# The first stage of an encoder trunk: norm by token, inputs on two queues, idle products, and a second home for modulation weights

## The chip, the core and the metric

The kernel runs on one core of one Trainium2 chip. The time is the device time of one execution in microseconds; a kernel's time is the median over its runs. The profile is of one such execution. Engines are named as in the profile: PE (TensorE, matrix products), PEld (its weight loads), DVE (VectorE), ACT (ScalarE), POOL (GpSimd), SP (SyncE, which issues most of the transfers).

## What is computed

The input is x (256 frames of 1024 channels) and a vector c of 1024. Two layers follow, each of three sub-layers: a SwiGLU feed-forward of 2816, a mixer (pooling in layer 0, short convolution in layer 1), and a second feed-forward. Each sub-layer is wrapped by a norm and a modulation that depends on c. All is float32.

```python
def rms_norm(x, g):
    y = xf * lax.rsqrt(jnp.mean(xf * xf, axis=-1, keepdims=True) + RMS_EPS)
    return (y * g).astype(x.dtype)

cond = jax.nn.silu(c)
for i in range(DEPTH):
    mod = (cond @ ada_w[i] + ada_b[i]).reshape(B, N_SUB, N_MOD, D_MODEL)
    shift, scale, gate = mod[:, :, 0], mod[:, :, 1], mod[:, :, 2]
    h = rms_norm(x, norm_g[i, 0]) * (1 + scale[:, 0]) + shift[:, 0]
    x = x + 0.5 * gate[:, 0] * swiglu(h, ffn_w_in[i, 0], ffn_w_out[i, 0])
    ...
return rms_norm(x, final_g)
```

## The kernel before

**Layout.** Channels lie on the 128 partitions, in 8 blocks (`KB`), and frames along the row: `x[:, k]` is block k of all 256 frames. All weights come from one array, `wall`, in units of 128 x 2048 float32 (1 MB), in the order in which the program asks for them. `raw_unit` takes a slot of a pool (tag `raw`, `NRAW` = 4 slots; a few units go to other tiles under tags of their own, `hi` and `lo`) and issues one transfer from SyncE (line 199). SyncE works through its transfers in order: each waits until its slot has been read for the last time, and all behind it wait with it. So SyncE runs ahead of the other engines by as many units as there are slots.

**Products in three parts.** A weight unit is split into two float32r tiles: `high` copies the unit to `hi` on ScalarE (line 239), `low` subtracts it again on VectorE to get `lo` (line 246). The activations are split likewise, into `hh` and `hl`. `mm3` makes one product of float32 quality out of three fast ones: hi with hh, lo with hh, hi with hl. `high(n)` and `low(n)` see to it that n units ahead of the one in use are split; `take` hands out the next one. The order of the work on each engine is the order of the program, written out by hand (`manual_schedule`).

**Modulation.** A modulation value is a dot product of a weight row with `cond`, made on VectorE (line 262, one dot for 128 channels, 1024 elements a partition). `mod_dots` makes the dots of a unit and finishes them (1 + scale times norm_g, half a gate). `ada_first(kb)` fetches the unit with scale and shift of block kb for the first sub-layer. All other modulation units go through `ada_unit`: `spread` deals them out over the steps of a feed-forward, and `slot` or `ada_next` fetches and works off one.

**The first stage** (lines 873 to 889 and `ffn_start`, from line 582). Four parts of x are squared on ScalarE into the buffer `hf` (8 blocks of 257 columns) and added on VectorE; cond is spread over the partitions by two products and put through Silu. `rstd_of` sums the squares over the partitions with a 128 x 256 product, takes the root on ScalarE and the reciprocal of 128 x 256 elements on VectorE (line 334). Then eight rounds follow, one for each block of the sum over channels. Round kb makes the block's modulation (two dots), forms h in `modulated` (t = x * scale * rstd on VectorE, line 359; t + shift on ScalarE, line 360; hl on VectorE, line 361), splits the block's weight unit in two halves (lines 618 and 623), and adds 48 products to eight PSUM banks, which hold 8 of the 22 column pairs of the first feed-forward. Round 0 takes its weight and its h unsplit, in plain float32, 16 products; its split into hh and hl is made in round 1. The second half of a round's `lo` and its products are put behind the dots of the next round (`second`).

**Behind it** all eight banks are full. `swiglu_pair` (from line 555: Silu on ScalarE, product gf and its split on VectorE) frees them two by two; product 8 needs the first. Column pairs 8 to 21 follow, one unit and 48 products each, then the second matrix (11 units, `out_product`), with the modulation units of the later part dealt out in between. `hf` isn't used from the end of the rounds until `pool_shift_by_token`, late in `out_product`, where the pooling mixer begins to use it.

Of the kernel before, what the change touches and what calls it, by code (L numbers as in the profile page):

```python
# [9 lines left out]
F32 = mybir.dt.float32  # L10
F32R = mybir.dt.float32r
AF = mybir.ActivationFunctionType
ALU = mybir.AluOpType
# [104 lines left out]
def trunk(ctx: ExitStack, tc: tile.TileContext, calls, consts: bass.AP, c_in: bass.AP,  # L118
# [16 lines left out]
    def mm(dst, w, m, start, stop):  # L135
        PE.matmul(dst, w, m, start=start, stop=stop, skip_group_check=True)  # L136
# [10 lines left out]

    eps = one.tile([P, LEAD], F32, name="eps")[:, :1]
    G.memset(eps, EPS)
    cond = one.tile([P, D], F32, name="cond")  # L150
    nc.sync.dma_start(cond[0:1], c_in)
    x = one.tile([P, KB, T], F32, name="x")
    for p in range(4):
        at = slice(2 * p, 2 * p + 2)
        nc.sync.dma_start(x[:, at], x_in[:, at])
# [23 lines left out]
    def table(func):  # L179

        tabs.append(wk.tile([P, 1], F32, tag="tab", name=f"tab{len(tabs)}"))
        S.activation(tabs[-1], eps, func)
# [9 lines left out]
    gh = one.tile([P, FC, T], F32R, name="gh")  # L192
    gl = one.tile([P, FC, T], F32R, name="gl")

    def raw_unit(*call, tag="raw"):
        u = len(calls)
        calls.append(call)
        t = wp.tile([P, UNIT], F32, tag=tag, name=f"raw{u}", bufs=NRAW if tag == "raw" else NSPLIT)
        nc.sync.dma_start(t, wall[u])
        return t  # L200
# [34 lines left out]
    def high(n, parts=1):  # L235

        for _, raw, hi, _ in next_of("hi", n):
            for at in spans(parts) if hi else ():
                S.copy(hi[:, at], raw[:, at])  # L239

    def low(n, parts=1):

        high(n, parts)
        for _, raw, hi, lo in next_of("lo", n):
            for at in spans(parts) if hi else ():
                V.tensor_sub(lo[:, at], raw[:, at], hi[:, at].bitcast(F32))  # L246
# [17 lines left out]
    def mod_dots(layer, sub, mod, w, lo):  # L264

        key, n = (layer, sub, mod), w.shape[1]
        if key not in mods:
            mods[key] = one.tile([P, KB], F32, name=f"mod{layer}{sub}{mod}")
        b = ada_col(layer, sub, mod) + lo
        for i in range(n):  # L270
            dot(mods[key][:, lo + i : lo + i + 1], w[:, i], cst[:, b + i : b + i + 1])
        mod_finish(key, lo, n)

    def mod_finish(key, lo, n):
# [7 lines left out]
        elif mod == GATE and layer == 0:  # L282
            V.tensor_mul(m, m, cst[:, C_PS + lo : C_PS + lo + n])

    def ada_unit(layer, sub, mod, q):
# [3 lines left out]
    def ada_first(kb):  # L289
        raw = raw_unit("ada0", kb).rearrange("p (m n) -> p m n", m=2)  # L290
        mod_dots(0, 0, SCALE, raw[:, 0:1], kb)
        mod_dots(0, 0, SHIFT, raw[:, 1:2], kb)

    ada_todo = []
    slots = {}
# [58 lines left out]
    def modulated(layer, sub, k, rstd, to):  # L354


        scale, shift = (mods[layer, sub, m][:, k : k + 1] for m in (SCALE, SHIFT))
        t = wk.tile([P, T], F32, tag="t", name=f"t{layer}{sub}{k}", bufs=4)
        V.scalar_tensor_tensor(t, x[:, k], scale, rstd, ALU.mult, ALU.mult)
        S.activation(to[:, k, :T], t, AF.Identity, bias=shift)  # L360
# [205 lines left out]
    def swiglu_early(pds, rstd, name, split):  # L566
        for at in range(0, len(pds), 2):
# [11 lines left out]
            for c in cs:  # L579
                V.tensor_sub(gl[:, c], ab[c][1][0], gh[:, c].bitcast(F32))  # L580

    def ffn_start(rstd, name):

        banks = [bank(f"{name}b{c}") for c in range(NFIRST)]
        half = NFIRST // 2

        def product(kb, w, cs):
            for c in cs:
                for s in range(2):
                    mm3(banks[c][:, s], (w[0][:, c, s], w[1][:, c, s]), h_pair(kb),  # L590
                        kb == 0 and s == 0, kb == KB - 1)

        second = lambda: None
        for kb in range(KB):
            if kb:
                ada_first(kb)
            call, raw, hi, lo = unit(kb)
            if hi is None:
                modulated(0, 0, kb, rstd, hf)
                second()  # L600
                low(1)
                w = take("ffn_first", "p (c s n) -> p c s n", c=NFIRST, s=2)
# [4 lines left out]
                def second(kb=kb):  # L607
                    S.copy(hh[:, kb, :T], hf[:, kb, :T])
                    V.tensor_sub(hl[:, kb], hf[:, kb, :T], hh[:, kb, :T].bitcast(F32))

                continue
            low_part = modulated(0, 0, kb, rstd, hh)
            second()
            low_part()
            high(1, 2)
            done["lo"] += 1
            at, bt = spans(2)
            V.tensor_sub(lo[:, at], raw[:, at], hi[:, at].bitcast(F32))
            w = take("ffn_first", "p (c s n) -> p c s n", c=NFIRST, s=2)
            product(kb, w, range(half))  # L620

            def second(kb=kb, w=w, raw=raw, hi=hi, lo=lo):
                V.tensor_sub(lo[:, bt], raw[:, bt], hi[:, bt].bitcast(F32))
                product(kb, w, range(half, NFIRST))

        second()
# [101 lines left out]
    def pool_means():  # L728
        S.copy(mh[:, :, 0, :EDGE], cst[:, C_E:C_M].rearrange("p (g v) -> p g v", g=4))
# [5 lines left out]
        V.tensor_mul(acc[:, :, :n], acc[:, :, :n], at)  # L735

    def pool_shift_by_token():
        pool_means()
# [133 lines left out]

    table(AF.Silu)
    sq2 = [hf[:, 2 * p : 2 * p + 2, :T] for p in range(4)]
    for p in range(4):
        S.activation(sq2[p], x[:, 2 * p : 2 * p + 2], AF.Square)
        if p:
            V.tensor_add(sq2[0], sq2[0], sq2[p])
    for p in range(2):
        b = bank(f"c{p}").rearrange("p a t -> p (a t)")  # L880
        half = slice(p * 512, (p + 1) * 512)
        PE.matmul(b, ones[0:1], cond[0:1, half], start=True, stop=True)
# [3 lines left out]
    V.tensor_add(sqs["a"], sq2[0][:, 0], sq2[0][:, 1])  # L886
# [79 lines left out]
```

## Time and profile before

| what | us |
| --- | --- |
| median of 3 runs | 863.17 |
| the runs | 862.32, 863.17, 872.11 |
| the profiled execution | 863.46 |
| its span, first to last instruction | 861.5 |

How to read the rows. A row of the timeline has the start and length in us, the engine, the line of the kernel, the operation, what it writes and reads (by tile names, without buffer numbers), and in brackets how long the engine sat idle before it and what ended that. A row of the waits reads: who waited, for whom, us in total, times, longest. A row of the windows has a stretch, its length, and for each engine the busy time with the number of instructions in it. The chain that ended last is followed back from the last instruction: at each step to what released it. The transfers of the weights have one line, 199, written `raw<-wall`. A busy PE isn't PE at its peak: the ends of its products are modelled, so their starts are what counts.

### The profile page before, as it was taken

Reading aid. Unit: us, or ns where it says so; the run is one execution under the profiler, and the core shown is the slowest. Engines: PE = TensorE matmul, PEld = TensorE weight load, DVE = VectorE, ACT = ScalarE, POOL = GpSimd, SP = SyncE. Lnnn points to the kernel's source line nnn. Section 1 sums busy time; section 2 is a strip of 40 time slices with the busy share of each in tenths; the row PEclk is TensorE's granted clock in tenths of the full one; section 3 lists DMA queues with packets and bytes.
Section 4 is the critical chain, followed back from the end, with each engine's and each line's share of the span. In section 5 each row is a group of like instructions: output and inputs, shape, how many; then the busy total and the mean of one; then the engine's idle time right before and its main releaser. Section 6 shows DMA issues by size and latency. Waiting matters only on the chain.

```text
span 861.5 us, 16344 instructions
## 1 busy us (share of the span) xinstructions
PE 841.8 (98%) x6940; PEld 822.8 (96%) x6940; DVE 714.6 (83%) x1018; ACT 418.3 (49%) x538; POOL 8.4 (1%) x25
## 2 busy tenths in 40 slices
PE   4999999999999999999999999999999999999997
PEld 2999999999899999999999999999999999999886
DVE  6989999877889987878888988879887789755784
ACT  5355455343655444446644444356444756444422
POOL 3000000000000000000000000000000000000000
PEclk9999999999999999999999999999999999999999
DMA  8898899989548998886389989983465449954601
GB/s 343 335 344 322 301 350 379 370 347 385 178 165 320 372 341 321 350 310 237 105 331 350 377 310 337 363 321 148 161 228 180 190 145 343 331 192 165 224 22 49
DMA packets 33338, 235.59 MB, mean 273 GB/s; under 512 B 3697, under 2 KB 3825, under 8 KB 4978
## 3 DMA queue, kind: packets, MB, share of 16 engines
q1 hardware_dynamic: 33266, 234.56, 73.6%
q8 instruction: 54, 0.88, 0.4%
q14 instruction: 18, 0.15, 0.0%
HBM read 233.49 MB, written 1.05 MB: 272 GB/s over the span
## 4 chain that ended last, share of the span: by engine, by line
PE 85%; DVE 7%; DMA 5%; ACT 1%; issue 1%; SPq 0%; ACTq 0%
PE accf L136 21%; PE f01b L136 13%; PE f10b L136 13%; PE f11b L136 11%; PE acco L136 7%; PE f00b L136 4%; DMA raw<-wall 4%; PE pcv L136 4%; DVE raw L262 3%; PE accc L136 3%; DVE lo L246 2%; PE pe L136 2%; PE pb L136 2%; PE f01a L136 1%; PE f11a L136 1%; PE accz L136 1%
## 5 line engine op out<-in xcount | busy, mean ns | idle before, releaser
L239 ACT CAST hi<-raw 128x2048 fp32r<-128x2048 f32 (+1 forms) x151 | 263.9, 1762 | 132.5 <-DMA raw<-wall 77.5
L246 DVE TENSOR_TENSOR lo<-raw,hi 128x2048 fp32r<-128x2048 f32 (+1 forms) x137 | 298.9, 2194 | 33.1 <-ACT hi L239 32.9
L262 DVE CUSTOM_DVE_ANT_0 raw<-raw,cond,cst 128x1024 f32<-128x1024 f32 x144 | 179.6, 1281 | 12.5 <-DMA raw<-wall 12.2
L136 PE MATMUL accf<-gh,hi 128*128 128x256 f32 x528 | 145.9, 276 | 0.0
L136 PE MATMUL accf<-gh,lo 128*128 128x256 f32 x528 | 145.9, 276 | 0.0
L136 PE MATMUL accf<-gl,hi 128*128 128x256 f32 x528 | 145.8, 276 | 0.0
L136 PEld LDWEIGHTS accf<-gh,lo 128*128 128x128 f32 x528 | 99.1, 188 | 0.2
L136 PEld LDWEIGHTS accf<-gh,hi 128*128 128x128 f32 x528 | 99.1, 188 | 0.0
L136 PEld LDWEIGHTS accf<-gl,hi 128*128 128x128 f32 x528 | 99.1, 188 | 0.0
L136 PE MATMUL f00b<-hh,lo 128*128 128x256 f32 x336 | 93.1, 277 | 1.2 <-DVE lo L246 0.8
L136 PE MATMUL f00b<-hh,hi 128*128 128x256 f32 x336 | 93.1, 277 | 0.4 <-DVE gf L560 0.4
L136 PE MATMUL f00b<-hl,hi 128*128 128x256 f32 x336 | 92.8, 276 | 0.0
L136 PE MATMUL f11b<-hh,lo 128*128 128x256 f32 (+1 forms) x320 | 88.5, 277 | 0.3 <-DVE lo L246 0.3
L136 PE MATMUL f11b<-hh,hi 128*128 128x256 f32 (+1 forms) x320 | 88.4, 276 | 0.0
L136 PE MATMUL f11b<-hl,hi 128*128 128x256 f32 x320 | 88.4, 276 | 0.0
L136 PE MATMUL f10b<-hh,lo 128*128 128x256 f32 x320 | 88.3, 276 | 0.0
L136 PE MATMUL f10b<-hh,hi 128*128 128x256 f32 x320 | 88.3, 276 | 0.0
L136 PE MATMUL f10b<-hl,hi 128*128 128x256 f32 x320 | 88.3, 276 | 0.0
L136 PE MATMUL f01b<-hl,hi 128*128 128x256 f32 x304 | 84.6, 278 | 0.0
L136 PE MATMUL f01b<-hh,hi 128*128 128x256 f32 x304 | 84.2, 277 | 0.0
L136 PE MATMUL f01b<-hh,lo 128*128 128x256 f32 x304 | 83.9, 276 | 0.0
L136 PEld LDWEIGHTS f00b<-hh,lo 128*128 128x128 f32 x336 | 63.1, 188 | 1.8 <-DVE lo L246 1.0
(234 smaller groups left out, 1856.5 us busy)
## 6 DMA issues: line engine op xcount, KB each, us to landing
raw<-wall SPq DMA_DIRECT2D x221, 1024.0 KB, 6.0
x<-xt SPq DMA_DIRECT2D x4, 256.0 KB, 4.1
out<-x SPq DMA_DIRECT2D x4, 256.0 KB, 2.1
rows<-fg SPq DMA_DIRECT2D x1, 512.0 KB, 8.3
cst<-consts SPq DMA_DIRECT2D x1, 176.0 KB, 4.8
cond<-cvec SPq DMA_DIRECT2D x1, 4.0 KB
```

What stands on the lines that cost most here:

```text
L136: PE.matmul(dst, w, m, start=start, stop=stop, skip_group_check=True)
L239: S.copy(hi[:, at], raw[:, at])
L246: V.tensor_sub(lo[:, at], raw[:, at], hi[:, at].bitcast(F32))
L262: V.tensor_tensor_reduce(w, w, cond, 1.0, init, ALU.mult, ALU.add, out)
```

## The change

1. **Inputs on two queues.** The parts of x with odd numbers and the constants are issued by ScalarE, the others by SyncE as before.
2. **Squares.** Two of the four parts are squared on VectorE. The four are added pairwise.
3. **Norm by token.** `rstd_by_token` makes the sum of squares with two one-column products, so that root and reciprocal have one column for 128 frames. The result is brought back along the row: a diagonal matrix (made once on GpSimd, scaled on ScalarE) is multiplied by `ones` (1/1024, against the 1024 on the diagonal) into a PSUM bank.
4. **x over rms by itself.** `normalised` multiplies x by rstd into `hf`: block 0 before the rounds, the other seven in four operations in round 0. `modulated_first` then makes scale and shift in one operation on ScalarE, in place; `split_first` makes hh and hl. The operation t on VectorE is gone.
5. **Order of a round.** First half of hi on ScalarE; the dots; Identity and hh on ScalarE; second half of hi; on VectorE the first half of lo, hl, products, second half of lo, products. Nothing is put off to the next round. hh and hl of block 0 are made at the end of round 1.
6. **Idle products.** `keep_busy` puts 8, 2 and 3 products of 128 columns, whose result isn't used, between the steps of the norm.
7. **Tables.** The Silu table, once loaded behind the norm's root, is loaded behind the rounds.
8. **Modulation units in hf.** From the end of the rounds to `pool_shift_by_token`, every second modulation unit goes to the first 2048 columns of `hf` instead of a slot.

```diff
     for p in range(4):
         at = slice(2 * p, 2 * p + 2)
-        nc.sync.dma_start(x[:, at], x_in[:, at])
+        (nc.scalar if p % 2 else nc.sync).dma_start(x[:, at], x_in[:, at])
     cst = one.tile([P, C_N], F32, name="cst")
-    nc.sync.dma_start(cst, consts)
+    nc.scalar.dma_start(cst, consts)
...
+    def home():
+        if not spare["on"]:
+            return None
+        spare["turn"] += 1
+        return hf.rearrange("p k t -> p (k t)")[:, :UNIT] if spare["turn"] % 2 else None
+
     def ada_unit(layer, sub, mod, q):
-        raw = raw_unit("ada", layer, sub, mod, q).rearrange("p (b n) -> p b n", b=2)
+        raw = raw_unit("ada", layer, sub, mod, q, home=home()).rearrange("p (b n) -> p b n", b=2)
         mod_dots(layer, sub, mod, raw, 2 * q)
...
+    def normalised(ks, rstd):
+        n = ks.stop - ks.start
+        at = bass.AP(rstd.tensor, rstd.offset, [rstd.ap[0], [0, n], rstd.ap[1]])
+        V.tensor_mul(hf[:, ks, :T], x[:, ks], at)
+
+    def modulated_first(k):
+        scale, shift = (mods[0, 0, m][:, k : k + 1] for m in (SCALE, SHIFT))
+        S.activation(hf[:, k, :T], hf[:, k, :T], AF.Identity, bias=shift, scale=scale)
+
+    def split_first(k):
+        S.copy(hh[:, k, :T], hf[:, k, :T])
+        return lambda: V.tensor_sub(hl[:, k], hf[:, k, :T], hh[:, k, :T].bitcast(F32))
...
         for kb in range(KB):
             if kb:
-                ada_first(kb)
+                w_ada = ada_first_weights(kb)
             call, raw, hi, lo = unit(kb)
+            at, bt = spans(2)
+            if hi is not None:
+                S.copy(hi[:, at], raw[:, at])
+            if kb:
+                for m, mod in enumerate((SCALE, SHIFT)):
+                    mod_dots(0, 0, mod, w_ada[:, m : m + 1], kb)
+            modulated_first(kb)
...
             if hi is None:
...
+                for ks in (slice(1, 2), slice(2, 4), slice(4, 6), slice(6, 8)):
+                    normalised(ks, rstd)
                 continue
...
+            low_part = split_first(kb)
+            S.copy(hi[:, bt], raw[:, bt])
+            V.tensor_sub(lo[:, at], raw[:, at], hi[:, at].bitcast(F32))
             low_part()
...
             product(kb, w, range(half))
+            V.tensor_sub(lo[:, bt], raw[:, bt], hi[:, bt].bitcast(F32))
+            product(kb, w, range(half, NFIRST))
+            if kb == 1:
+                split_first(0)()
+
+        spare["on"] = True
+        table(AF.Silu)
         low(1)
         high(2)
...
+    squares(0)
+    squares(1)
     for p in range(2):
...
         PE.matmul(b, ones[0:1], cond[0:1, half], start=True, stop=True)
+        if p == 0:
+            squares(2)
         S.activation(cond[:, half], b, AF.Silu, scale=float(D))
     table(AF.Sqrt)
+    squares(3)
+    idle = bank("idle")
+
+    def keep_busy(n):
+        for _ in range(n):
+            PE.matmul(idle[:, 0, :P], ones, ones, start=True, stop=True)
+
+    keep_busy(8)
+    V.tensor_add(sq2[1], sq2[1], sq2[0])
+    V.tensor_add(sq2[3], sq2[3], sq2[2])
+    V.tensor_add(sq2[1], sq2[1], sq2[3])
     sqs["a"] = wk.tile([P, T], F32, tag="sq", name="sqs", bufs=3)
-    V.tensor_add(sqs["a"], sq2[0][:, 0], sq2[0][:, 1])
-    rstd = rstd_of("s")
-    table(AF.Silu)
-    ada_first(0)
+    V.tensor_add(sqs["a"], sq2[1][:, 0], sq2[1][:, 1])
+    w_first = ada_first_weights(0)
+    mod_dots(0, 0, SCALE, w_first[:, 0:1], 0)
+
+    by_token_rstd = rstd_by_token("s")
+    mod_dots(0, 0, SHIFT, w_first[:, 1:2], 0)
+    keep_busy(2)
...
+    for b in range(2):
+        cut = slice(b * P, (b + 1) * P)
+        S.activation(diag[:, cut], unit_matrix, AF.Copy, scale=by_token_rstd[:, b : b + 1])
+        PE.matmul(rstd[:, cut], ones, diag[:, cut], start=b == 0, stop=True, skip_group_check=True)
+    keep_busy(3)
+    normalised(slice(0, 1), rstd)
```

More of the change, by code (lines that the diff above doesn't have):

```diff
@@ L149, in trunk @@
     G.memset(eps, EPS)
+    unit_matrix = wk.tile([P, T], F32, tag="sa", name="unit")[:, :P]
+    G.memset(unit_matrix, 0.0)
+    G.affine_select(unit_matrix, unit_matrix, [[-1, P]], ALU.not_equal, float(D), base=0, channel_multiplier=1)
     cond = one.tile([P, D], F32, name="cond")
@@ L193, in trunk, with raw_unit @@
     gl = one.tile([P, FC, T], F32R, name="gl")
-    def raw_unit(*call, tag="raw"):
+    def raw_unit(*call, tag="raw", home=None):
         u = len(calls)
         calls.append(call)
+        if home is not None:
+            nc.sync.dma_start(home, wall[u])
+            return home
         t = wp.tile([P, UNIT], F32, tag=tag, name=f"raw{u}", bufs=NRAW if tag == "raw" else NSPLIT)
@@ L283, in mod_finish, with ada_first_weights @@
             V.tensor_mul(m, m, cst[:, C_PS + lo : C_PS + lo + n])
+    spare = {"on": False, "turn": 0}
+    def home():
[3 more added lines that the diff above has]
+        return hf.rearrange("p k t -> p (k t)")[:, :UNIT] if spare["turn"] % 2 else None
     def ada_unit(layer, sub, mod, q):
-        raw = raw_unit("ada", layer, sub, mod, q).rearrange("p (b n) -> p b n", b=2)
+        raw = raw_unit("ada", layer, sub, mod, q, home=home()).rearrange("p (b n) -> p b n", b=2)
         mod_dots(layer, sub, mod, raw, 2 * q)
[L289 to L292, printed above, removed]
+    def ada_first_weights(kb):
+        return raw_unit("ada0", kb).rearrange("p (m n) -> p m n", m=2)
     ada_todo = []
@@ L591, in product @@
                         kb == 0 and s == 0, kb == KB - 1)
-        second = lambda: None
         for kb in range(KB):
             if kb:
-                ada_first(kb)
+                w_ada = ada_first_weights(kb)
             call, raw, hi, lo = unit(kb)
+            at, bt = spans(2)
[5 more added lines that the diff above has]
+            modulated_first(kb)
+            done["hi"] += 1
+            done["lo"] += 1
+            w = take("ffn_first", "p (c s n) -> p c s n", c=NFIRST, s=2)
             if hi is None:
[L599 to L602, printed above, removed]
                 for c in range(NFIRST):
@@ L874, in trunk, with squares @@
     sq2 = [hf[:, 2 * p : 2 * p + 2, :T] for p in range(4)]
[L875 to L878, printed above, removed]
+    def squares(p):
+        xp = x[:, 2 * p : 2 * p + 2]
+        if p % 2:
+            V.tensor_mul(sq2[p], xp, xp)
+        else:
+            S.activation(sq2[p], xp, AF.Square)
+    squares(0)
+    squares(1)
     for p in range(2):
@@ L882, in trunk @@
         PE.matmul(b, ones[0:1], cond[0:1, half], start=True, stop=True)
+        if p == 0:
+            squares(2)
         S.activation(cond[:, half], b, AF.Silu, scale=float(D))
     table(AF.Sqrt)
[L885 to L889 removed]
+    squares(3)
[7 more added lines that the diff above has]
+    V.tensor_add(sq2[1], sq2[1], sq2[3])
+    sqs["a"] = wk.tile([P, T], F32, tag="sq", name="sqs", bufs=3)
+    V.tensor_add(sqs["a"], sq2[1][:, 0], sq2[1][:, 1])
[4 more added lines that the diff above has]
+    keep_busy(2)
+    diag = wk.tile([P, T], F32, tag="sd", name="diag", bufs=1)
+    rstd = bank("rstds")[:, 0]
+    for b in range(2):
[4 more added lines that the diff above has]
+    normalised(slice(0, 1), rstd)
     steady = [4] * (LAST - 2)
```

15 lines of the change are left out of this document (1 added, 14 removed).

## The prediction, made before the changed kernel was run

> **What bounds the kernel now.** I read the page first, then the waits of PE, then the chain that ended last in order of time.
>
> ```profile
> PE 841.8 (98%) x6940; PEld 822.8 (96%) x6940; DVE 714.6 (83%) x1018; ACT 418.3 (49%) x538; POOL 8.4 (1%) x25
> ```
> ```profile
> PE f00b L136 <- ACT hf L360: 5.8, 1, 5.8
> ...
> PE f00b L136 <- DVE lo L246: 0.8, 1, 0.8
> PE f00b L136 <- DVE gf L560: 0.4, 1, 0.4
> PE f00b L136 <- DVE lo L623: 0.4, 1, 0.4
> ```
> ```profile
> 88.40 2.30 DVE lo L246
> 90.75 7.07 DMA raw<-wall
> ...
> 104.69 38.27 PE f00b L136 x335
> ```
> Lines are start, length and what the time went to. From 104.69 us the chain is PE, stage after stage; ahead of it fetches (DMA raw<-wall) and VectorE alternate. What the change can win is therefore the time until PE begins, what PE loses while it runs slowly, and the three waits before 105 us. Whatever arrives earlier at 105 us arrives earlier at the end, as long as VectorE and the fetches keep up.
>
> PE's own pace is seen in two stretches of the first product block (32 records, f00b<-hf,raw) and in one behind it (columns: the stretch and its length, PE and PE's weight loads with the records in it, the granted clock, the DMA engines' busy share, GB/s; the third stretch has VectorE and ScalarE between):
>
> ```profile
> 16.46:20.89 4.43, 4.43 (x10) 3.53 (x11) 1.00 1.03 436
> 21.27:25.59 4.32, 4.32 (x22) 3.80 (x21) 1.00 0.75 305
> ```
> ```profile
> 26.04:55.90 29.86, 29.86 (x264) 29.76 (x263) 0.00 (x0) 0.00 (x0) 1.00 0.93 343
> ```
> The granted-clock column says 1.00 throughout, yet the same instruction takes 0.43 us in the first stretch (4.43/10) and 0.216 in the second (20 begin in it). The slow start costs some 2.3 us. Behind it one fp32r product takes 29.86/263 = 0.1135 us, so a round of 48 takes PE 5.45 us.
>
> **The start, step by step.** Before:
>
> ```profile
> 2.42 3.75 PE L882 MATMUL c<-cond,ones 1*128 1x512 f32 x4 [2.42 <-DMA cond<-cvec]
> ...
> 3.50 56.19 SPq L199 DMA_DIRECT2D raw<-wall  x20
> ...
> 5.96 0.69 DVE L878 TENSOR_TENSOR hf<-hf 128x512 f32<-128x512 f32 x1 [2.88 <-ACT hf L876]
> ...
> 7.46 0.63 ACT L876 ACTIVATE hf<-x 128x512 f32<-128x512 f32 x1 [0.20 <-DMA x<-xt]
> ...
> 8.86 0.53 DVE L886 TENSOR_TENSOR sqs<-hf 128x256 f32<-128x256 f32 x1
> 9.07 1.28 ACT L182 ACT_TABLE_LOAD   x1
> ...
> 11.21 1.75 DVE L334 RECIPROCAL rstds<-sds 128x256 f32<-128x256 f32 x1 [1.82 <-ACT sds L333]
> ...
> 15.79 1.28 DVE L262 CUSTOM_DVE_ANT_0 raw<-raw,cond,cst 128x1024 f32<-128x1024 f32 x1
> 15.90 0.51 ACT L360 ACTIVATE hf<-t,mod 128x256 f32<-128x256 f32 x1 [3.21 <-DVE t L359]
> ...
> 19.32 0.39 ACT L608 CAST hh<-hf 128x256 fp32r<-128x256 f32 x1
> ```
> ```profile
> 1.21 1.78 SPq L155 DMA_DIRECT2D x<-xt  x4
> ```
> ```profile
> 211.53 0.17 DVE L345 RECIPROCAL rqp<-rtp 128x2 f32<-128x2 f32 x1 [1.79 <-ACT rtp L343]
> ```
> Inputs: SyncE issues four parts of x in 1.78 us (0.45 each); the last square starts at 7.46 when its part lands. With two parts on ScalarE's queue the last part is issued about 0.9 us sooner. The trace shows no second queue. Bounds for the landing: 7.4 (the transfer, not the issue, was the limit) and 6.1 (the issue time of two parts and of the constants, 1.3 us, all won). I take 6.6, near the issue time of the two parts alone; with 7.4 all that follows, the forecast too, would be 0.8 us later. The three issues on ScalarE (1.3 us) lie under its wait for x. The stream of weights moves up as well: SyncE's first raw goes out at about 2.1 instead of 3.50.
>
> The Trainium skill, "DMA: Bandwidth & Descriptors", section "Issuing engines are not separate DMA queues", says that several issuing engines save only the issue time, because all transfers share the same 16 DMA engines. By that rule the landing is 6.5 at the earliest; no run here has a second queue yet that could show it.
>
> Squares: VectorE squares part four (0.69, by the add of the same shape), then adds three times, two of them one behind the other, and folds (0.53): 6.6 + 0.7 + 0.65 + 0.7 + 0.7 + 0.55 = 9.9. That is 0.5 later than the 9.39 of before. The eight idle products (a quarter of the columns of line 882's, which took 0.94 a record, two records each: 0.43 to 0.47) end by 9.9 in the worst case, so they don't hold the sum of squares up. The first modulation unit is there too (2.1 + 7.6, the median fetch quoted with the rounds below). ScalarE's Sqrt table is in by then: two squares, two Silus and a load of 1.28 from 6.6 on. Norm by token: two one-column products and the root, until 10.9 (estimate); the reciprocal has 2 columns, 0.17 instead of 1.75, but stands behind the SCALE dot on VectorE (9.9 to 11.35): 11.5. The SHIFT dot then runs until 12.8, and beside it two ScalarE copies to the diagonal (no row at 128x128; 0.2 for one column, 0.51 for 256: 0.3 each) and two 128-column products: rstd is there at 12.9. First multiplication by rstd 0.4, Identity 0.51: the first product begins at **13.9** instead of 16.46, 2.5 us earlier. The other idle products stand on PE between these steps: two from 10.6 to 11.5, before the diagonal is there, and three behind the rstd products, which at the slow pace would hold PE until 14.3; what hides those 0.4 us comes below.
>
> VectorE then multiplies the other seven blocks in one go: 0.4 + 3 x 0.65 (0.69 in the row, reading PSUM; all four between 1.9 and 2.8). Its next dot, the first of round 1, begins at **15.75**. Before it was 15.79. So PE starts sooner, but VectorE has gained nothing yet.
>
> The two GpSimd operations for the diagonal's pattern cost nothing: what is made behind them, the band matrix, is first read in the pooling layer, some 200 us later, and the pattern itself is wanted at 11.5.
>
> **The rounds.** Before, one round on VectorE:
>
> ```profile
> 27.57 1.28 DVE L262 CUSTOM_DVE_ANT_0 raw<-raw,cond,cst 128x1024 f32<-128x1024 f32 x1
> ...
> 30.18 0.48 DVE L359 SCALAR_TENSOR_TENSOR t<-x,mod,rstds 128x256 f32<-128x256 f32 x1
> 30.57 1.22 DVE L623 TENSOR_TENSOR lo<-raw,hi 128x1024 fp32r<-128x1024 f32 x1
> ...
> 32.18 1.23 DVE L618 TENSOR_TENSOR lo<-raw,hi 128x1024 fp32r<-128x1024 f32 x1
> 33.33 1.28 DVE L262 CUSTOM_DVE_ANT_0 raw<-raw,cond,cst 128x1024 f32<-128x1024 f32 x1
> ...
> 58.11 1.22 DVE L623 TENSOR_TENSOR lo<-raw,hi 128x1024 fp32r<-128x1024 f32 x1
> ```
> ```profile
> raw<-wall SPq DMA_DIRECT2D x11, 1024.0 KB, 7.6
> ```
> That is 5.76 us a round. The change takes t away (0.39) but loses its cover: the second half's lo of the former round used to stand between the dots and hl; now both halves of lo belong to the same round, and the second half of hi comes on ScalarE behind Identity (0.51), the copy to hh (0.39, the row of line 608 at 19.32) and its own 1.0. Dots end at 2.69 of the round, ScalarE is through at 2.69 + 1.95, then lo 1.14: **5.8**. The fetch loop says the same: a slot is released at the end of lo, the fetch of two rounds later takes 7.6 (median of the eleven fetches between 30 and 60 us), and hi, Identity, hh, hi, lo take 4.05 behind it: 11.65 for two rounds, 5.8. One hl for block 0 adds 0.43. The last lo ends at 15.75 + 0.43 + 7 x 5.8 = **56.8**; before it was 59.3.
>
> PE: 13.9 + 32 x 0.216 + 7 x 5.45 = 59.0, or 61.2 if the idle products don't hold the fast pace; by VectorE 56.8 + 24 x 0.1135 = 59.5.
>
> **Behind the rounds** nothing of this decides, but the first swiglu pair, which frees the PSUM bank of product 8:
>
> ```profile
> 62.70 1.92 ACT L239 CAST hi<-raw 128x2048 fp32r<-128x2048 f32 x1 [2.99 <-DMA raw<-wall]
> 64.52 0.64 ACT L558 ACTIVATE saf<-f00b 128x256 f32<-128x256 f32 x2
> ```
> ```profile
> 65.39 0.39 PE L136 MATMUL f00b<-hh,hi 128*128 128x256 f32 x1 [0.42 <-DVE gf L560]
> ```
> ```profile
> 31.82 8.63 DMA raw<-wall
> ...
> 55.08 7.51 DMA raw<-wall
> ```
> Silu stood behind the hi of unit 9, which waited for a fetch issued at 55.08. Now that fetch is issued at the end of round 6's lo, 51.0, with two others in flight: 8.2 (estimate, between its 7.5 and the 8.6 of the chain's piece at 31.82), so 59.2. ScalarE: round 7's hi ends at 55.6, the Silu table now loads here (1.28 + 0.1), hi of unit 8 until 58.9, hi of unit 9 59.2 to 61.1, Silu 0.4, the multiplication 0.42: product 8 begins at **62.0** instead of 65.39, **3.4 us** earlier. PE waits some 2.5 us for it; that hides the idle products' gain entirely.
>
> **The hf buffer.** The last wait:
>
> ```profile
> 104.69 0.39 PE L136 MATMUL f00b<-hh,lo 128*128 128x256 f32 x1 [0.81 <-DVE lo L246]
> ```
> ```profile
> 83.88 1.28 DVE L262 CUSTOM_DVE_ANT_0 raw<-raw,cond,cst 128x1024 f32<-128x1024 f32 x1 [0.71 <-DMA raw<-wall]
> ...
> 97.84 1.28 DVE L262 CUSTOM_DVE_ANT_0 raw<-raw,cond,cst 128x1024 f32<-128x1024 f32 x1 [1.35 <-DMA raw<-wall]
> ```
> ```profile
> 60.00:120.00 60.00, 58.77 (x515) 58.38 (x515) 52.52 (x76) 30.76 (x42) 0.00 (x0) 1.00 0.88 318
> 120.00:160.00 40.00, 40.00 (x353) 39.86 (x352) 39.05 (x54) 19.26 (x22) 0.00 (x0) 1.00 0.99 380
> ```
> VectorE waits for a modulation fetch (0.71, then 1.35), which was issued only when the lo at 88.40 had freed its slot; lo of unit 15 is late by as much. These are the third and the fifth modulation unit of the part, and both go to hf now: the fifth needs only the third's dots done, at 86.4 before, so it can be issued up to 4 us sooner. SyncE's queue issues in order, so the units behind an hf fetch wait with it; at the first one hf is free when round 7's hl is done (55), before the next slot (56.8). The fetches moved 318 GB/s between 60 and 120 us and 380 later, so there is room. Gain: the **0.8** of the PE row. Beyond it VectorE (the third pair of columns: 39.05 of 40 us busy) must stay ahead; by these terms it is 3.4 + 0.7 + 1.35 ahead of its old times. Without the gain, PE would meet the same late lo 3.4 us earlier and wait 0.8 again.
>
> **Sum.** 3.4 + 0.8 = 4.2. The profiled execution took 863.46 (span 861.5 and 2.0 around it): 859.3. It lies 0.3 above the median of the three runs, 863.17, so **859.0** for a median; the rivals' times are against the median too. A measurement tells about 2%, 17 us, from no change; this is far below it.
>
> **Rivals.**
> *Later wait stays* (18%): hf fetches are held up in SyncE's order; the 0.8 is lost: 859.8. For it: 0.99 DMA share from 120 us. Against it: 0.88 before.
> *PE alone sets the time* (10%): fetches come soon enough that no wait is left: 2.5 + 2.3 + 0.4 + 0.4 + 0.8 = 6.4: 856.8. It needs the warm pace at 13.9; against it stand 5.8 for VectorE's round over PE's 5.45.
> *Fetches pace the stage* (17%): at 343 GB/s a unit takes 3.05 us, a round 6.1, and the stream starts only 1 to 1.3 us sooner (first raw at 3.5); product 8 wins 1.3, the later wait stays: 861.9. Against it: 436 GB/s early on.
> *ScalarE's new order backfires* (8%, slower): hi stands ahead of Identity now, so a late weight fetch holds up the dots' result too. By the loop above a round is (fetch + 4.05)/2; with 9.4 a fetch it is 6.7, 0.9 over 5.8, and seven of them end 6.3 later: 3.4 + 0.8 - 6.3 = 2.1 slower: 865.3. It decides from 8.75 us a fetch (a round 0.6 longer); one of the chain's pieces (8.63) comes near, the median of 7.6 does not.
> That the idle products fail to raise the pace would cost nothing while 61.2 stays below 62.0.
>
> **Chances.** Forecast 47%, and the rivals as given. The range 856.4 to 862.4 leaves out the slower one and the tails. Faster by over 2%: 0.01; within: 0.98; slower: 0.01.
>
> **What would show it.** The first product near 13.9 at 0.216 a record; VectorE's rounds 5.8; a new PE wait of 2 to 3 us for gf near 62, larger than the 0.4 of before; no wait for lo near 100; the chain all PE from there. Wrong it would be if the rounds took over 6.2, if product 8 began after 64, or if PE waited for lo between 100 and 160.

## The result, and the profile after

The changed kernel takes **859.44 us** (median of 16 runs, 858.77 to 860.01); the kernel before 863.62 (16 runs, 861.31 to 872.14). The ratio of the runs is 0.9931, 95% interval 0.9908 to 0.9955. By the medians that is 4.2 us, by the two profiled spans 3.9 (861.5 to 857.6). The ratio alone would make it some 6 us, because the runs of the kernel before reach up to 872.14 and those of the changed one don't.

The page's first line and the waits of PE on the products, as before:

```profile
PE 845.7 (99%) x6972; PEld 827.5 (96%) x6972; DVE 713.2 (83%) x1017; ACT 421.8 (49%) x545; POOL 9.4 (1%) x27
```
```profile
PE f00b L136 <- DVE gf L575: 0.9, 1, 0.9
...
PE f11b L136 <- DVE lo L253: 0.3, 1, 0.3
```
Of the four waits before 105 us one is left, the one for gf, and it has grown from 0.4 to 0.9. The chain that ended last, in order of time, shows what ends it:

```profile
2.08 8.09 DMA raw<-wall
...
54.82 0.61 ACT hf L605
55.77 1.04 ACT hi L644
56.83 1.28 ACT L186
58.23 1.91 ACT hi L246
60.16 2.29 DVE lo L253
62.84 76.45 PE f00b L136 x672
```
PE now carries the chain from 62.84 us on, where it took until 104.69 before. Ahead of it stand round 7 on ScalarE, the Silu table, hi of unit 8 and its lo; the multiplication that frees PSUM follows on VectorE (62.37). The chain begins with the fetch of the first modulation unit, issued at 2.08 and landed 8.1 us later. Now the start:

```profile
6.28 3.42 PE L929 MATMUL idle<-ones 128*128 128x128 f32 x16
...
6.63 0.69 DVE L908 TENSOR_TENSOR hf<-x 128x512 f32<-128x512 f32 x1 [1.44 <-DMA x<-xt]
...
7.34 0.63 ACT L910 ACTIVATE hf<-x 128x512 f32<-128x512 f32 x1 [1.38 <-DMA x<-xt]
...
8.08 0.92 DVE L933 TENSOR_TENSOR hf<-hf 128x512 f32<-128x512 f32 x1
...
10.34 1.43 DVE L269 CUSTOM_DVE_ANT_0 raw<-raw,cond,cst 128x1024 f32<-128x1024 f32 x1
...
11.99 0.15 DVE L360 RECIPROCAL rqs<-rts 128x2 f32<-128x2 f32 x1
...
12.69 1.22 PE L948 MATMUL rstds<-diag,ones 128*128 128x128 f32 x4 [1.08 <-ACT diag L947]
...
13.71 1.49 PE L929 MATMUL idle<-ones 128*128 128x128 f32 x6
13.95 2.54 DVE L601 TENSOR_TENSOR hf<-x,rstds 128x256 f32<-128x256 f32 x5 [0.62 <-PE rstds L948]
14.46 0.60 ACT L605 ACTIVATE hf<-hf,mod,mod 128x256 f32<-128x256 f32 x1 [1.53 <-DVE hf L601]
...
16.41 1.28 DVE L269 CUSTOM_DVE_ANT_0 raw<-raw,cond,cst 128x1024 f32<-128x1024 f32 x1
```
```profile
15.12 7.60 PE L136 MATMUL f00b<-hf,raw 128*128 128x256 f32 x32
22.36 0.47 PE L136 MATMUL f00b<-hh,hi 128*128 128x256 f32 x1
```
The first product begins at 15.12, round 1's dots at 16.41, round 1's products at 22.36. And a round on VectorE, from one dot to the next round's, with the fetches between 23 and 53 us:

```profile
34.42 1.28 DVE L269 CUSTOM_DVE_ANT_0 raw<-raw,cond,cst 128x1024 f32<-128x1024 f32 x1
...
37.02 1.22 DVE L645 TENSOR_TENSOR lo<-raw,hi 128x1024 fp32r<-128x1024 f32 x1
38.22 0.43 DVE L609 TENSOR_TENSOR hl<-hf,hh 128x256 fp32r<-128x256 f32 x1
39.17 1.23 DVE L648 TENSOR_TENSOR lo<-raw,hi 128x1024 fp32r<-128x1024 f32 x1 [0.53 <-ACT hi L644]
40.31 1.28 DVE L269 CUSTOM_DVE_ANT_0 raw<-raw,cond,cst 128x1024 f32<-128x1024 f32 x1
```
```profile
raw<-wall SPq DMA_DIRECT2D x10, 1024.0 KB, 5.5
```
A round takes 5.89 us, 0.53 of it waiting for the second half of hi.

### The profile page after: what moved, and what is told of

Its sections match the earlier page's. It is cut to its first block, busy times and chain, and to the rows that moved or that the text cites. A ratio compares the mean times of both kernels' runs of the same rounds, so it can differ in the third digit from the quotient of the medians.

```text
span 857.6 us, 16417 instructions
## 1 busy us (share of the span) xinstructions
PE 845.7 (99%) x6972; PEld 827.5 (96%) x6972; DVE 713.2 (83%) x1017; ACT 421.8 (49%) x545; POOL 9.4 (1%) x27
## 4 chain that ended last, share of the span: by engine, by line
PE 90%; DVE 6%; ACT 3%; DMA 1%; issue 0%; SPq 0%; ACTq 0%; DVEq 0%
PE accf L136 21%; PE f01b L136 13%; PE f10b L136 13%; PE f11b L136 11%; PE f00b L136 9%; PE acco L136 7%; PE pcv L136 4%; PE accc L136 3%; DVE raw L269 2%; PE pe L136 2%; PE pb L136 2%; PE f01a L136 1%; DVE lo L253 1%; DMA raw<-wall 1%; DVE lo L648 1%; PE f11a L136 1%
## 5 line engine op out<-in xcount | busy, mean ns | idle before, releaser
L246 ACT CAST hi<-raw 128x2048 fp32r<-128x2048 f32 (+1 forms) x137 | 249.9, 1835 | 126.0 <-DMA raw<-wall 61.2
L269 DVE CUSTOM_DVE_ANT_0 raw<-raw,cond,cst 128x1024 f32<-128x1024 f32 x126 | 157.4, 1282 | 6.3 <-DMA raw<-wall 6.1
L136 PEld LDWEIGHTS f00b<-hh,hi 128*128 128x128 f32 x336 | 63.1, 188 | 1.4 <-DVE gf L575 1.1
```

The costliest lines, as they stand in the source:

```text
L269: V.tensor_tensor_reduce(w, w, cond, 1.0, init, ALU.mult, ALU.add, out)
```

## The experiments

None of these kernels ran beside the changed kernel itself. Its 859.44 comes from another set of runs, in which the kernel before had 863.62; in the three sets below the kernel before had 863.18, 862.70 and 863.89, and for every kernel up to 860.9 below that is a variant of the changed one, the interval of the ratio overlaps with the changed kernel's. So differences from 859.44 of up to about 1 us are differences of medians, and the rows of one profiled execution say where they would come from.

**Which part gives what.** First part 8 alone, on the kernel before; then the change without part 8 (the line `spare["on"] = True` left out).

```diff
+        if home is not None:
+            nc.sync.dma_start(home, wall[u])
+            return home
...
-        raw = raw_unit("ada", layer, sub, mod, q).rearrange("p (b n) -> p b n", b=2)
+        raw = raw_unit("ada", layer, sub, mod, q, home=home()).rearrange("p (b n) -> p b n", b=2)
```


> The kernel before with part 8 alone: every second modulation unit goes to hf. Theory (a late modulation fetch delays lo of unit 15, nothing else): the 0.8 us PE wait for lo near 104.7 us is gone, product 8 still begins near 65.4 us, the span falls by 1.0 to 1.3 us (the wait, 0.97 from start to start, and some 0.3 of smaller ones behind it), to about 860.3 us. Rival (the wait only moves, or hf fetches hold up the queue): PE still waits for lo between 95 and 160 us and the span stays within 0.4 us of 861.5. Also open: the runs of the kernel before spread from 861 to 872 us and those of the changed one only from 858.8 to 860.0; if the spread comes from late fetches behind the rounds, this kernel's runs spread no wider than 2 us.

Measured: 861.68 (12 runs, 860.75 to 863.16), 863.18 for the kernel before beside it, ratio 0.9975 (0.9955 to 0.9994); the profiled span is 859.5. No wait for lo of unit 15 is left, and the span is 2.0 below 861.5, so the rival falls. But the gain is 1.5 to 2.0, not 1.0 to 1.3, and product 8 didn't begin at 65.4: in this execution the multiplication in front of it came two us earlier than the 64.92 of before,

```profile
62.98 0.75 DVE L571 TENSOR_TENSOR gf<-saf,f00b 128x256 f32<-128x256 f32 x2 [0.87 <-ACT saf L569]
```
so that PE was still busy with round 7. Whether hf does that or the fetch only came sooner in this one execution isn't shown. The runs spread over 2.4 us, a little more than the 2 that were asked about, where the 29 runs of the kernel before beside them spread over 9.7 (861.25 to 870.9).

```diff
-        spare["on"] = True
         table(AF.Silu)
```


> The changed kernel with all modulation units in the slots again, the rest as changed. Theory: product 8 still begins near 62.8 us, but PE waits for lo of unit 15 near 101 us again, span 858.4 to 858.9 us (0.8 to 1.3 over 857.6). Rival (the wait is gone because the first stage ends earlier, not because of hf): no PE wait near 101 us, span within 0.3 us of 857.6.

Measured: 860.88 (12 runs, 858.86 to 863.69), ratio 0.9958 (0.9937 to 0.9979), span 860.2. The wait near 101 us is back, so the rival falls, and a second one came with it. Product 8 began at 63.55 here, not near 62.8, and the span lies above what the theory gave, 858.4 to 858.9.

```profile
102.76 0.39 PE L136 MATMUL f00b<-hh,lo 128*128 128x256 f32 x1 [0.72 <-DVE lo L253]
```
```profile
152.59 0.38 PE L136 MATMUL accf<-gh,lo 128*128 128x256 f32 x1 [0.55 <-DVE lo L253]
```
Without hf the earlier first stage loses 0.7 and 0.55 again downstream. So hf is worth 1.4 on top of the rest (860.88 against 859.44) and 1.5 alone; the first stage is worth 2.3 alone (863.18 against 860.88).

**Idle products.**

```diff
-    keep_busy(8)
...
-    keep_busy(2)
...
-    keep_busy(3)
```


> The changed kernel without its 13 idle products. Theory: round 0 runs at the slow pace (0.43 us a record) for its first 4 us or more and ends near 24.3 instead of 22.4 us, but the rounds behind it are set by VectorE and product 8 by ScalarE's chain, so product 8 begins within 0.2 us of 62.8 and the span is within 0.3 us of 857.6. Rival (the pace of PE at the start counts): the span is 1.5 to 2.3 us longer.

Measured: 859.46 (8 runs, 858.90 to 860.81), span 857.8. For the time the theory holds; round 0 ended at 22.91, though, not at 24.3. The first product even begins 0.44 earlier:

```profile
14.68 1.22 PE L136 MATMUL f00b<-hf,raw 128*128 128x256 f32 x2 [1.21 <-ACT hf L605]
```
```profile
PE f00b L136 <- DVE gf L575: 0.8, 1, 0.8
```
```profile
DVE lo L645 <- ACT hi L628: 1.1, 3, 0.5
```
That isn't the idle products' doing. Part four of x landed earlier in this execution (its square began at 6.16, against 6.63), and in both kernels the product begins 0.05 to 0.06 us behind Identity's end. The lead was gone by product 8, which began at 62.98: in three rounds VectorE waited for the first half of hi (the last row, between 22 and 60 us), and that for its weights.

**Inputs on one queue.**

```diff
-        (nc.scalar if p % 2 else nc.sync).dma_start(x[:, at], x_in[:, at])
+        nc.sync.dma_start(x[:, at], x_in[:, at])
...
-    nc.scalar.dma_start(cst, consts)
+    nc.sync.dma_start(cst, consts)
```


> The changed kernel with x and the constants issued by SyncE alone, as before. In the changed kernel the last part of x landed at 7.32 us, as before (the last square began at 7.46 there). Theory (the transfer, not the issue, sets x's landing): x lands within 0.3 us of 7.4, the weights start 1.4 us later (first raw 3.5), round 1's dots begin within 0.4 us of 16.4 and the span is within 0.4 us of 857.6. Rival (the two queues gained what the prediction says, 0.8 us): the span is 0.8 us or more longer.

Measured: 860.12 (10 runs, 859.77 to 860.44), 0.7 more, span 858.6. My theory falls (round 1's dots began 1.0 later), the rival is close. Part four, which VectorE squares, is what the second queue brings forward:

```profile
7.71 0.69 DVE L908 TENSOR_TENSOR hf<-x 128x512 f32<-128x512 f32 x1 [1.64 <-DMA x<-xt]
...
17.40 1.27 DVE L269 CUSTOM_DVE_ANT_0 raw<-raw,cond,cst 128x1024 f32<-128x1024 f32 x1
```
Its square began at 6.63 in the changed kernel, and round 1's dots at 16.41. I had looked at the part that landed last (7.3 with two queues), but that is now one that ScalarE squares, beside VectorE's chain of adds. In the eleven profiled executions with two queues part four's square began between 6.0 and 6.6 and part three's, the last, between 7.0 and 8.2; in four of them VectorE did wait for part three, for 0.5 to 1.3 us.

**Norm by row.** The changed kernel with the old norm:

```diff
-    by_token_rstd = rstd_by_token("s")
+    rstd = rstd_of("s")
     mod_dots(0, 0, SHIFT, w_first[:, 1:2], 0)
...
-    rstd = bank("rstds")[:, 0]
-    for b in range(2):
...
```


> The changed kernel with the norm by row as before (a 128 x 256 product, root and reciprocal of 128 x 256), the rest as changed. Theory (the 1.75 us reciprocal stands on VectorE between the two dots, and VectorE sets all up to product 8): the first product begins near 16.2 instead of 15.1 us, round 1's dots near 17.5 instead of 16.4, and the median rises by 1.0 to 860.5. Rival (fetches set the rounds, the start is absorbed): median within 0.4 of 859.4.

Measured: 860.27 (6 runs, 859.82 to 861.07), 0.8 more, span 858.5. The theory holds:

```profile
12.09 1.75 DVE L349 RECIPROCAL rstds<-sds 128x256 f32<-128x256 f32 x1
13.75 1.19 DVE L269 CUSTOM_DVE_ANT_0 raw<-raw,cond,cst 128x1024 f32<-128x1024 f32 x1
...
17.34 1.28 DVE L269 CUSTOM_DVE_ANT_0 raw<-raw,cond,cst 128x1024 f32<-128x1024 f32 x1
```
**The table, and the order on ScalarE.**

```diff
             modulated_first(kb)
+            if kb == 0:
+                table(AF.Silu)
...
         spare["on"] = True
-        table(AF.Silu)
```


> The changed kernel, with the Silu table loaded on ScalarE in round 0 (where it waits 2.5 us for a fetch) instead of behind the rounds. Theory (product 8 waits for ScalarE's chain: round 7's hi, table load 1.28 + 0.1, hi of units 8 and 9, Silu): product 8 begins 1.1 to 1.4 us earlier, near 61.7 instead of 62.8, just as PE is through with the rounds, and the median falls by 1.1 us to 858.3. Rival (the fetch of unit 9, which landed at 58.2, takes the table's place): product 8 begins 0 to 0.4 us earlier, median 859.1 to 859.4.

Measured: 858.40 (6 runs, 857.51 to 859.20), 862.70 for the kernel before beside it, ratio 0.9943 (0.9927 to 0.9959); span 856.9. By the medians 1.0 lower, as the theory has it; the wait for gf shrinks from 0.9 to 0.4. In the profiled execution product 8 came only 0.6 earlier (62.2): there ScalarE waited 0.95 for unit 9 before its hi at 59.52, as the rival has it, so the profile stands between the two.

```diff
                 S.copy(hi[:, at], raw[:, at])
+                S.copy(hi[:, bt], raw[:, bt])
...
-            S.copy(hi[:, bt], raw[:, bt])
             V.tensor_sub(lo[:, at], raw[:, at], hi[:, at].bitcast(F32))
```


> The changed kernel, with the second half of hi copied on ScalarE ahead of the dots, not behind Identity and hh. Theory (the round of 5.89 us holds 0.53 of waiting for that copy): rounds of 5.36 us on VectorE, so PE's 5.45 sets the pace, rounds end on PE near 60.6 instead of 61.7, product 8 begins right then without a wait, median 857.2 (2.2 lower). Rival (the fetch loop gives 5.8 a round by itself, as the prediction worked out): rounds stay at 5.7 to 5.9 and the median within 0.5 of 859.4.

Measured: 859.28 (6 runs, 857.27 to 859.98; the lowest is at the theory's time): by the median my theory falls and the rival holds. What VectorE waits for between 22 and 58 us in the changed kernel, and between 22 and 60 here:

```profile
DVE lo L648 <- ACT hi L644: 3.7, 7, 0.5
```
```profile
DVE lo L253 <- ACT hi L246: 1.8, 1, 1.8
DVE hl L609 <- ACT hh L608: 1.7, 3, 0.7
DVE lo L645 <- ACT hi L628: 1.3, 2, 0.8
```
The seven waits of 0.53 are gone, but in two rounds the weights now land after the dots, hi comes late, and hh behind it: rounds of 5.3 and of 6.5 to 6.9 take turns, 5.93 in the mean of rounds 2 to 6 (first dots at 22.15 and 51.81). No wait for gf is left in front of product 8.

> Both edits: table in round 0 and second half of hi ahead of the dots. Theory: with rounds paced by PE nothing waits for ScalarE's chain any more, so it equals the kernel with the hi edit alone within 0.2 us, 857.2. Rival (product 8 still waits for ScalarE there): another 0.5 to 1.1 us lower.

Measured: 858.51 (6 runs, 856.63 to 859.02). Lower than the hi edit alone by 0.8, and equal to the table alone: the rival's number. Its mechanism isn't seen, for in neither profiled execution (858.09 and 857.71) does product 8 wait for gf. In the profiled one of both edits PE waits for nothing from round 1 to product 8, and VectorE's rounds 2 to 6 took 5.53 in the mean (22.82 to 50.49).

> Both edits, without the 13 idle products. Theory (idle products are worth nothing only while VectorE and ScalarE set the pace; here PE does): slower than with them by what round 0's end moves in the changed kernel without them, 22.9 instead of 22.4 us: 0.4 to 0.6 us. Rival (still hidden): within 0.2 us of it.

Measured: 858.93 (6 runs, 858.24 to 859.63), 0.4 more, at the edge of what was expected; the runs overlap, so it isn't shown that the idle products count here.

**GpSimd beside VectorE.** The changed kernel with the band matrix built late (its lines as a function `bands`):

```diff
-        lambda u: u == LAST - 3 and pool_shift_by_token(), rstd=rstd)
+        lambda u: (u == 1 and bands(), u == LAST - 3 and pool_shift_by_token()), rstd=rstd)
```


> The changed kernel with the building of the band matrix (GpSimd, and a clearing on VectorE) put behind the first unit of the second matrix. In the changed kernel VectorE's adds took 0.92, 0.92 and 0.80 us beside GpSimd's selects of 0.77, where they took 0.69 and 0.43 apart. Theory (the two slow each other): the adds take 0.69 each, the SCALE dot 1.28 instead of 1.43, round 1's dots begin 0.6 us earlier, near 15.8, and the median falls by 0.5 to 858.9. Rival (they are slow for another reason, or x's landing sets the chain): adds stay above 0.8, median within 0.2 of 859.4.

Measured: 859.26 (6 runs, 858.83 to 859.98), 0.2 less, span 857.5. The theory holds for the durations and fails for the time:

```profile
8.49 0.69 DVE L937 TENSOR_TENSOR hf<-hf 128x512 f32<-128x512 f32 x1 [0.79 <-ACT hf L914]
9.22 0.69 DVE L938 TENSOR_TENSOR hf<-hf 128x512 f32<-128x512 f32 x1
...
16.30 1.28 DVE L273 CUSTOM_DVE_ANT_0 raw<-raw,cond,cst 128x1024 f32<-128x1024 f32 x1
```
The adds take 0.69, but the second now waits 0.79 for ScalarE's square of the part that lands last, and the SCALE dot 0.23 for its fetch. Some 0.5 of the 0.79 is a later landing in this execution (that square began at 7.83, against 7.34), so the profile alone doesn't settle it; the median shows no clear gain either, as the rival's second half (x's landing sets the chain) has it. The Trainium skill, "SBUF — State Buffer", section "Who interferes with whom", says that a VectorE instruction with two inputs in SBUF and a GpSimd instruction that reads SBUF use one shared port, and that the later one waits. The durations of these runs agree that the two slow each other: 0.92 against 0.69 for the adds, 0.77 against 0.43 for the selects. Which of the two waited isn't shown.

**Other slots for the rounds.** On top of the table and hi edits, the modulation units of the rounds in the tag `lo`. Its four slots aren't free: the expectation below calls them slots of their own, but the lo tiles of the weight units use them too.

```diff
-        return raw_unit("ada0", kb).rearrange("p (m n) -> p m n", m=2)
+        return raw_unit("ada0", kb, tag="lo" if kb else "raw").rearrange("p (m n) -> p m n", m=2)
```


> Table in round 0, second half of hi ahead of the dots, and the modulation units of rounds 1 to 7 in slots of their own (the four of tag lo), so that the four raw slots hold weight units alone. Theory (with both edits the rounds of 5.3 to 6.9 us are uneven because of the fetch loop): rounds of 5.3 to 5.5 us, no wait of PE from the first round to product 8, median 857.0 to 857.6, against 858.5 without the slots. Rival (the fetches' rate, 2 MB a round, sets the rounds whatever the slots): rounds of 5.8 or more, median 858.2 to 858.6.

> The kernel with slots of its own for the modulation units, table in round 0 and hi ahead of the dots, and the band matrix built late as well. Theory (PE now sets everything from round 1 on, so an earlier start comes through): another 0.4 to 0.6 us lower than without the late band matrix, 856.5 to 857.1. Rival (the fetches of the first weight units set the start of round 1): within 0.2 us of it.

Measured: 864.30 (12 runs, 858.60 to 873.54), ratio 0.998 (0.9953 to 1.0007), and, with the late band matrix, 867.70 (12 runs, 857.84 to 874.64), ratio 1.0019 (0.9992 to 1.0046). Both theories and both rivals fail for the time. For the rounds the first rival holds: 5.90 on VectorE in the mean of rounds 2 to 6 (22.14 to 51.65). The edit also brought a new wait: up to 70 us SyncE's queue stood 21.0 us behind PE's products, in four waits, because PE is the last to read a slot of that tag. So it doesn't show what slots of their own would give. In the profiled execution of the first PE waits for nothing from round 1 to product 8, as hoped, and yet the span is 866.2: the same products run slower. Three stretches of the changed kernel, then of this one (columns as in the prediction: the stretch, its length, PE and its weight loads with their records, the granted clock, the DMA share, GB/s):

```profile
25.00:45.00 20.00, 20.00 (x178) 19.94 (x177) 1.00 0.94 360
...
150.00:180.00 30.00, 30.00 (x267) 30.00 (x266) 1.00 0.88 348
260.00:280.00 20.00, 20.00 (x178) 20.00 (x178) 1.00 0.96 358
```
```profile
25.00:45.00 20.00, 20.00 (x172) 20.00 (x172) 1.00 0.83 316
...
150.00:180.00 30.00, 30.00 (x257) 30.00 (x256) 1.00 0.73 286
260.00:280.00 20.00, 20.00 (x179) 20.00 (x178) 1.00 0.90 317
```
From 150 to 180 us 265 products begin in the one, 255 in the other (the windows also count those under way at their start): one every 0.1133 us against one every 0.1178. More on that below.

## Why the prediction was right, point by point

859.0 was forecast and 859.44 came, 4.2 us of gain and 4.2. But the two terms of the sum were each off by about 1, in opposite directions, and that the total fits so closely is luck.

**The first stage: 3.4 forecast, 2.3 to 2.55 measured** (without hf against before; product 8 at 62.84 instead of 65.39). Two sizes were off, about equally: the start by 0.66 (round 1's dots at 16.41, not 15.75) and the seven rounds by 0.09 each, so that the last lo ended at 58.1, not 56.8. Some of that came back behind the rounds. For the start: the sum of squares was ready at 10.4 instead of 9.9: 6.6 was forecast for the last part to land, and part four did (its square began at 6.63), but part three, from SyncE, landed at 7.3; and the adds took 0.92, 0.92 and 0.80 beside GpSimd, not 0.7. An earlier sum would have helped little, for the first modulation unit landed at 10.2, not at 9.7. The SCALE dot and its finish took 1.65 instead of 1.45 up to the reciprocal, and from the reciprocal's end the diagonal and the two rstd products, at the slow pace, took 1.8 instead of 1.4; with the later sum, rstd came at 13.9, not 12.9. The first product began at 15.12, not 13.9, right behind Identity's end (14.46 + 0.60); that the last three idle products would hold it, as the working said they might, isn't seen.

**The rounds: 5.8 forecast, 5.89 measured**, for the reason given first: hi's second half behind Identity and hh, 0.53 of waiting a round. The second reason, the fetch loop, is nearly as tight. In this execution a fetch took 5.5, not the 7.6 taken over from before, and VectorE waited for none (ScalarE did, 9.2 us in seven waits, but with time to spare). In five other kernels with the same rounds a fetch took 7.2 to 7.4 (5.7 a round by the prediction's loop), and a lead at the start was lost to it in the kernel without idle products. With hi copied early the profiled rounds took 5.93, with the early table as well 5.53, and without idle products on top 6.13.

**Product 8** was forecast as waiting for ScalarE's chain, by way of unit 9's fetch, its hi and Silu. The table load does stand in the chain, and moving it to round 0 gave 1.0 by the medians; but the way from there was another. Unit 9 was there in time (ScalarE's two hi follow each other from 58.23 to 61.9), and the multiplication began when VectorE was through with lo of unit 8 (60.16 and 2.29). PE's wait was 1.1 (62.84 less 61.63 and a normal step), not 2.5, because PE itself was through only at 61.7, not 59.5. The prediction put 24 products behind the last lo; all but the first two of round 7's 48 stand behind its hl, which ended at 56.3, and 56.3 + 46 x 0.1135 = 61.5.

**Idle products** forecast as worth nothing: 0.0. They do raise the pace: round 0 took 7.2 us with them and 8.2 without (9.2 before). The prediction's 4.43/10 is 0.44, not 0.43; nothing hangs on it. **Norm by token** is 0.8 of the start, **the second queue** 0.7. The rule of the Trainium skill that the prediction quotes ("DMA: Bandwidth & Descriptors", "Issuing engines are not separate DMA queues") agrees: part four, issued second on its queue instead of fourth, was squared 1.1 earlier than with one queue (6.63 against 7.71), about what the issue saves, and the part that landed last did so at 7.3, no earlier than the 7.4 of before.

**hf: 0.8 forecast, 1.4 to 1.5 measured.** The wait at unit 15 is gone as said. What the term left out is the next wait in line, at 152 us, for lo of a unit of the second matrix. With the first stage earlier it would have cost 0.55; the prediction named VectorE's 39.05 of 40 us there and didn't price it. In the kernel before, where hf alone gave 1.5, that wait doesn't exist; there the rest of the gain stood in front of product 8, and whether it is hf's isn't shown.

The slower rival (ScalarE's new order) didn't come: it needed 8.75 us a fetch. PE alone setting the time (856.8) was the limit that the table and hi edits were to reach; both together reached 858.5, and the profiled execution, in which PE waited for nothing, took 857.71.

**A better version?** The table in round 0 alone has a median of 858.40, 1.0 below the changed kernel's 859.44. The two were timed beside different runs of the kernel before, and the intervals of the ratios overlap (0.9927 to 0.9959, 0.9908 to 0.9955), and by the ratios (0.9943 against 0.9931) it isn't lower at all. So it is lower by the medians, and not shown to be better.

## What to carry to other kernels

When a stage is moved forward, list the slack of every later unit, not only the waits that show: a unit whose operand is ready with nothing to spare is the next wait, and an extra buffer there can be worth more than the wait it removes, as hf was here. Price a start by the chain of dependent operations on each engine with what runs beside them, and by when that chain needs each part of an input, not by the last landing alone. A table load behind a stage is on the path if the next stage's first operation waits for that engine; put it where the engine waits for a transfer. And don't explain a fetch time by an edit before other executions with the same stage have been looked at.

## What the runs showed of the hardware that I had not expected

**Two lasting paces of PE.** The same products run at one per 0.1133 or one per 0.1178 us, 4% apart, for 170 us and more at a stretch, while the granted clock reads 1.00 in both and VectorE's durations don't change. In the profiled execution of the first kernel with slots of tag `lo` the slow pace lasts from round 1 to the second feed-forward, in the other one (with the late band matrix) it holds at 260 us and not at 150, and in both it is back from about 620 us to 800, but for some 15 us near 700. The last row is of the first kernel again:

```profile
150.00:180.00 30.00, 30.00 (x267) 30.00 (x266) 1.00 0.84 327
260.00:280.00 20.00, 20.00 (x172) 20.00 (x171) 1.00 0.98 365
```
```profile
640.00:660.00 20.00, 20.00 (x172) 20.00 (x172) 1.00 0.44 156
```
The first three feed-forwards keep one pace each, but for a few products at their ends: slow, fast, fast in the one execution, fast, slow, fast in the other. From 25 to 240 us alone 4% is some 8 us. What brings it about stays open: no run here varies it. The runs of one of these programs range from 858.6 to 873.5, so the program doesn't fix it, but in the profiled executions such stretches were seen only in the two kernels with slots of tag `lo`, and the other kernels with hf stay within 3 us in all their runs, two of them timed in the same set. The kernel before ranges as widely, from 861.3 to 872.1; its one profiled execution has the fast pace.

**The granted clock and the slow start.** In the kernel before the column read 1.00 over a stretch in which PE went at half its pace. In the changed kernel it shows the half, just ahead of round 0 and in its first records (columns as above):

```profile
12.70:15.90 3.20, 0.78 (x2) 0.69 (x3) 0.50 1.01 428
16.50:22.34 5.84, 5.84 (x29) 5.13 (x28) 1.00 0.99 407
```
PE had reached the fast pace once before, at 9.2 us, among the first eight idle products (their records were 0.111 us apart from there, 0.213 ahead of it). Between 9.5 and 12.4 us it was busy for 1.36 of 2.9 us, and the last three idle products, from 13.7, were back at 0.213.

**A fetch has no fixed time.** With the same four slots a unit landed 7.6 us after its issue in the rounds of before (median of eleven), 5.5 in those of the changed kernel (median of ten), and 7.2 with hi copied early:

```profile
raw<-wall SPq DMA_DIRECT2D x10, 1024.0 KB, 7.2
```
That isn't the hi edit's doing. The same view, between 23 and 53 us, gives 5.5 with the norm by row and 7.2 to 7.4 in five kernels whose rounds are those of the changed one (without hf, without idle products, one queue, early table, late band matrix); with both edits it gives 6.1. So a median fetch of one execution can be 2 us off in the next, while VectorE's rounds stay at 5.9 to 6.0. What decides it isn't shown, nor that the transfers in flight slow each other.
